# Attention heads on one core: key maxima a tile sooner, the row of -max in tile 6, the merge's last step in two halves

## The chip, the core and the metric

The kernel runs on one core of a Trainium2 chip. The core has five engines with instruction queues of their own: TensorE (PE, matmuls; its weight loads are shown as PEld), VectorE (DVE), ScalarE (ACT), GpSimd (POOL) and SyncE (SP, which here only issues DMAs). The engines run side by side and wait for each other by semaphores; each works through its own queue in order. The metric is the device time of one execution in microseconds (us). Before the change three runs took 3254.74, 3255.23 and 3263.18 us; the median is 3255.23 us.

## The reference, cut to what matters

The program is two whole transformer blocks for 1024 tokens of width 1024: a first block (a recurrent branch and a latent attention branch, then a mixture of experts) and a second (a gated linear recurrence and pooling, then another mixture of experts). The change lies in the attention of the first block. Its core is:

```python
def chunk_causal_attention(q, k, v):
    B, S, H, _ = q.shape                 # S = 1024, H = 16 heads, 96 per head
    scale = QK_HEAD ** -0.5
    outs = []
    for blk in range(S // Q_BLOCK):      # Q_BLOCK = 128
        q0 = blk * Q_BLOCK
        k_end = q0 + Q_BLOCK
        qb = q[:, q0:k_end]
        s = jnp.einsum('bqhd,bkhd->bhqk', qb, k[:, :k_end]).astype(jnp.float32) * scale
        ...                              # mask by chunks of 64
        s = jnp.where(mask, s, -jnp.inf)
        p = jax.nn.softmax(s, axis=-1).astype(v.dtype)
        outs.append(jnp.einsum('bhqk,bkhd->bqhd', p, v[:, :k_end]))
    return jnp.concatenate(outs, axis=1).reshape(B, S, H * V_HEAD)
```

Afterwards the block forms `merged = gates[:, :, 0] * ya + gates[:, :, 1] * yb`, where yb is this attention and ya the recurrent branch, and multiplies it by w_out.

## The kernel before

Everything is float32. A product is made of three matmuls, of operands split into a high and a low part (h and l in the names): high by high, high by low, low by high.

The attention takes the 16 heads one after the other, and each head in 8 key tiles of 128 keys (kt = 0 to 7). Scores are made transposed, with keys in the partitions: `s_mm` (L942) makes for one key tile the scores of all later queries, in pieces of up to 512 columns (tile `st`, three PSUM buffers), and ACT writes their exponential into `raw` (L952; three buffers). `s_split` (L954) makes of raw the high part `ph` (on ACT, for tile 0 on DVE) and on POOL the low part `pl` (L253; from 1024 columns for tile 0 down to 128 for tile 7; three buffers each). Three key tiles later, `av` (L960) multiplies them by the values and adds into two PSUM accumulators of 512 queries (`o`): for each piece it issues value-high by ph, value-low by ph and value-high by pl.

The maxima that the exponential needs are not taken from these scores. While head h is worked on, the next head n = h + 1 is prepared: `t_piece` (L896) transposes its keys and queries in tiles 0 and 1 (tile `tm` in PSUM, three buffers, which is shared by the next two), `m_piece` (L913) makes for a query tile i and 512 keys from a a plain score product (one matmul, L918), and DVE takes its maximum along the keys (L921, and L923 for the diagonal's last 64 keys) into `nm`. `row_piece` (L925) takes the largest of these per query with a minus sign (mz, L927), turns them into a row by eight small matmuls (L931), and ACT (L937) and DVE (L935) copy the row into the queries' tile, as one more contraction row. Then the scores come out with their maximum taken off, and so row_piece stands in front of all scores of head n. `v_piece` (L906) splits the values of head n: DVE the high part (vh, L251), POOL the low part (vl, L253).

The sums of the exponentials come out of the same accumulators. `finish` (L974) copies an accumulator half into y (L985 on DVE for the second half) and sends the row of sums through a small DMA; `rec` (L989) takes the reciprocals and brings them back, over DRAM, spread over 64 partitions, by the DMAs L995 and L998, into the tile `rec`. A pair of heads (2 pr and 2 pr + 1) shares one tile rec of 128 partitions, and the pool has a single buffer of that name: the tile for a new pair is asked for in `rec` of its even head. `merge` (L1000) then works on rec in six parts: parts 0 and 1 multiply by y for either head (POOL, L1006), part 2 takes in one gate (DVE, L1008), part 3 the recurrent branch (DVE, L1010), part 4 writes the high half of the result (ACT, L1013, two instructions), part 5 the low one (DVE, L1016, two instructions) and then starts the loads of the gates for the next pair (`gates`, L1023). When each part comes is in the table MERGE (L832): a first head and a key tile for each part, and then every second head. So part 0 is in tile 6 of odd heads, part 1 in tile 5 of even ones, parts 2 to 5 in tiles 0 to 3 of odd heads from 3 on, for the pair before.

The order is written out by hand. `line` (L1057) yields the units of one step: the pieces of s_mm for (h, kt), then those of av for three tiles earlier; after the last unit come `finish` and `s_split`. (In tile 0 of a head the av of the last head's tile 5 comes first.) `beside` (L1076) gives a list of fillers for that step, in this order: transposes, maxima, the values, the row, rec, the merge. The loop at L1106 to L1129 deals the fillers out evenly among the units:

```python
next(units)
for u in range(nu):
    next(units, None)
    for f, *a in fill[-(-len(fill) * u // nu):-(-len(fill) * (u + 1) // nu)]:
        f(*a)
```

so that how many fillers a step has decides behind which unit each of them comes, and whether it stands before or after the step's s_split.

Of the kernel before, what the change touches and what calls it, by code (L numbers as in the profile page):

```python
# [231 lines left out]
class Body:  # L232
# [601 lines left out]
    def attention(self, rb, rk, ml):  # L834
# [4 lines left out]
        with ExitStack() as cx:  # L839
# [14 lines left out]
            def load(pr):  # L854
                if pr >= 8:
                    return
                if pr not in L:
                    room(pr)
                c, o = pr // 2, pr % 2
                d = L[pr]  # L860
                for w, a in (("k", self.k_d), ("q", self.q_d)):
                    nc.sync.dma_start(d[w][:, :1536].rearrange("p (t c) -> p t c", t=8),
                                      a[c].rearrange("(t p) c -> p t c", p=128)[:, :, o * 192:o * 192 + 192])
                for i, w in enumerate("kq"):
                    nc.sync.dma_start(d[w][:, 1536:].rearrange("p (t c) -> p t c", t=4),
                                      self.v_d[c].rearrange("(t p) c -> p t c", p=128)
                                      [:, i * 4:i * 4 + 4, o * 128:o * 128 + 128])
# [208 lines left out]
            def beside(h, kt):  # L1076

                n = h + 1
                fill = []
                if kt == 0 and h % 2:  # L1080
                    load(h // 2 + 2)
                if n < 16:
                    if kt < 2:
                        fill += [(t_piece, n, "kq"[kt], half) for half in range(2)]
                    fill += [(m_piece, n, i, a) for i, a in
                             {3: [(7, 0), (7, 512), (6, 0)], 4: [(6, 512), (5, 0), (5, 512)],
                              5: [(4, 0), (4, 512), (3, 0)], 6: [(2, 0), (1, 0), (0, 0)]}.get(kt, ())]
                    if kt == 5:
                        fill.append((v_piece, n))
                    if kt == 7:  # L1090
                        fill.append((row_piece, n))
                if kt == 3 and h > 0:
                    fill.append((rec, h - 1))
                for part, (late, at) in enumerate(self.MERGE):
                    if h >= late and (h - late) % 2 == 0 and kt == at:
                        fill.append((merge, (h - late) // 2, part, 0, 2, nc.vector if h == 15 else nc.gpsimd))
                return fill

# [7 lines left out]
            for j in range(16 * 8 + 3):  # L1106
                if j == 13 * 8:
                    wo(0, 3)
                    wo(1, 2)
                if j == 14 * 8 + 6:  # L1110
                    wo(2, 1)
                    wo(3, 0)
                if j == 15 * 8 + 3:
                    rk.close()
                    co = rb.enter_context(tc.tile_pool(reuse_waits="tile", name="co", bufs=1, side="right"))
                    self.cols1 = co.tile([128, 8, 32, 6], BF, name="cols1")
                    wa = rk.enter_context(tc.tile_pool(reuse_waits="tile", name="wa", bufs=1, side="right"))
                if j == 128:
                    last(0)
                units = line(j)  # L1120
                fill = beside(j // 8, j % 8) if j < 128 else []
                if 15 * 8 + 4 <= j < 15 * 8 + 7:
                    fill.append((self.wo_split, wa, *((0, 0), (0, 1), (1, 0))[j - 124]))
                nu = sum(len(chunks(k)) for k in ([j % 8] if j < 128 else []) + ([(j - 3) % 8] if j >= 3 else []))
# [5 lines that stand above are left out]
# [1624 lines left out]
```

## Time and profile before

| | |
|---|---|
| median of three runs | 3255.23 us (3254.74 to 3263.18) |
| the profiled execution | 3259.96 us |
| its span in the profile | 3258.1 us |
| PE busy in the span | 2923.7 us, 90% |
| DVE, ACT, POOL busy | 2002.5, 1395.4, 988.0 us |
| granted TensorE clock, mean | 0.949 of full speed |

The heads of the attention run from about 742 to 1110 us after the start of the span. There each engine's idle time is put down to what ended it, and the time of one head can be read from one group of row matmuls (L931) to the next. PEclk is the share of full clock that TensorE was granted; its two levels are 1.2 and 2.4 GHz, so 0.50 is the lower one. Busy time of an engine that shares a resource with another can be longer than its work.

### The profile page before, as it was taken

The numbers are of one execution on the slowest core, as the hardware profiler recorded it, in microseconds if no ns is written. First come the engines' busy times: TensorE is split into PE (matmuls) and PEld (weight loads), VectorE is DVE, ScalarE is ACT, GpSimd is POOL, SyncE is SP. The second block draws the span as 40 slices with busy tenths as digits, with TensorE's granted clock in tenths as the row PEclk, the third lists the DMA queues.
The fourth block names the chain that finished last, engine by engine and source line by source line (L and its number), as shares of the span: only waits on it lengthen the run. The fifth ranks groups of instructions, "written<-read, shape, count | busy, mean of one in ns | idle before, by whom it ended". The sixth has DMA issues, their size and how long they took to land. (4 is left out here: it accounts for less than half of the span.)

```text
span 3258.1 us, 43717 instructions
## 1 busy us (share of the span) xinstructions
PE 2923.7 (90%) x16309; PEld 2268.3 (70%) x16309; DVE 2002.5 (61%) x3093; ACT 1395.4 (43%) x2096; POOL 988.0 (30%) x678
## 2 busy tenths in 40 slices
PE   5999999998888987899699998857999999999994
PEld 4778778886777885666488878845666666656563
DVE  5554651667877648998645566544655555555456
ACT  3333331545666424776443333332444444444342
POOL 0000000135777414564211132121333333222223
PEclk9999999998999997999899999978999999999997
DMA  3112120353232357999710003337989999999994
GB/s 113 65 56 81 65 88 7 120 163 99 75 88 91 115 204 228 342 349 347 245 52 27 27 17 101 110 128 226 278 278 318 320 322 314 312 310 314 298 287 139
DMA packets 225897, 579.84 MB, mean 178 GB/s; under 512 B 22421, under 2 KB 104005, under 8 KB 225653
## 3 DMA queue, kind: packets, MB, share of 16 engines
q1 hardware_dynamic: 188240, 445.42, 39.0%
q0 software_dynamic: 37008, 131.50, 16.2%
q8 instruction: 131, 2.15, 0.3%
q14 instruction: 86, 0.70, 0.1%
q10 hardware_dynamic: 432, 0.06, 0.0%
HBM read 470.22 MB, written 106.64 MB: 177 GB/s over the span
## 5 line engine op out<-in xcount | busy, mean ns | idle before, releaser
L271 PE MATMUL mm<-uh,wh 128*128 128x512 f32 x640 | 252.7, 395 | 10.8 <-ACT t L505 8.8
L272 PE MATMUL gups<-gl,xh 128*128 128x512 f32 (+1 forms) x608 | 246.9, 406 | 10.4 <-DVE gl L253 10.4
L271 PE MATMUL gups<-gh,xh 128*128 128x512 f32 (+1 forms) x608 | 254.5, 419 | 1.3 <-ACT xh L1594 0.9
L273 PE MATMUL mm<-uh,wl 128*128 128x512 f32 x640 | 251.8, 393 | 0.0
L272 PE MATMUL mm<-ul,wh 128*128 128x512 f32 x640 | 251.6, 393 | 0.0
L273 PE MATMUL gups<-gh,xl 128*128 128x512 f32 (+1 forms) x608 | 246.7, 406 | 0.4 <-DVE xl L1595 0.4
L1696 POOL DMA_INDIRECT acc_d<-y,si x68 | 119.3, 1755 | 408.0 <-DVE y L1693 175.7
L1480 PE MATMUL gups<-raw,x 128*128 128x512 f32 x512 | 226.7, 596 | 0.0
L253 POOL TENSOR_TENSOR pl<-raw,ph 128x1024 fp32r<-128x1024 f32 (+7 forms) x128 | 203.6, 1610 | 71.3 <-ACT ph L247 36.1
L253 DVE TENSOR_TENSOR gl<-raw,gh 128x1024 fp32r<-128x1024 f32 x185 | 217.9, 1219 | 8.0 <-ACT gh L247 7.9
L1627 ACT ACTIVATE th<-gups 128x128 f32<-128x128 f32 (+2 forms) x136 | 49.0, 360 | 349.1 <-PE gups L273 187.2
L247 ACT ACTIVATE gh<-raw 128x1024 fp32r<-128x1024 f32 x188 | 188.5, 1058 | 14.0 <-PE gups L273 12.7
L1584 PEld LDWEIGHTS tp<-ident,xg 128*128 128x128 f32 (+2 forms) x1088 | 112.5, 143 | 97.2 <-issue 36.4
L1691 ACT ACTIVATE y<-yps,wsl 128x512 f32<-128x512 f32 (+1 forms) x100 | 68.8, 688 | 253.1 <-PE yps L273 152.1
L1480 PEld LDWEIGHTS gups<-raw,x 128*128 128x128 f32 x512 | 96.4, 193 | 108.1 <-issue 108.1
L1628 DVE SCALAR_TENSOR_TENSOR hh<-th,gups 128x128 f32<-128x128 f32 (+2 forms) x136 | 52.9, 389 | 186.0 <-ACT th L1627 180.3
L1584 PE MATMUL tp<-ident,xg 128*128 128x128 f32 (+2 forms) x1088 | 128.2, 261 | 42.2 <-DMA xg<-h_d 27.7
L1693 DVE TENSOR_SCALAR y<-yps,wsl 128x512 f32<-128x512 f32 (+1 forms) x95 | 71.1, 748 | 137.5 <-ACT y L1691 137.5
L271 PEld LDWEIGHTS mm<-uh,wh 128*128 128x128 f32 x640 | 121.8, 190 | 38.0 <-ACT t L505 10.6
L272 PEld LDWEIGHTS gups<-gl,xh 128*128 128x128 f32 (+1 forms) x608 | 112.2, 184 | 43.1 <-issue 11.8
L273 PEld LDWEIGHTS mm<-uh,wl 128*128 128x128 f32 x640 | 121.6, 190 | 25.7
L272 PEld LDWEIGHTS mm<-ul,wh 128*128 128x128 f32 x640 | 121.7, 190 | 25.4
(681 smaller groups left out, 8204.3 us busy)
## 6 DMA issues: line engine op xcount, KB each, us to landing
raw<-in_w_down_dram SPq DMA_DIRECT2D x78, 1024.0 KB
raw<-in_w_gate_dram SPq DMA_DIRECT2D x154, 512.0 KB
raw<-in_w_up_dram SPq DMA_DIRECT2D x154, 512.0 KB
w<-in_w_in_dram SPq DMA_DIRECT2D x20, 1024.0 KB
b<-in_w_gate_dram SPq DMA_DIRECT2D x38, 512.0 KB
b<-in_w_up_dram SPq DMA_DIRECT2D x38, 512.0 KB
b<-in_w_down_dram SPq DMA_DIRECT2D x18, 1024.0 KB
w<-in_w_in_dram SPq DMA_DIRECT2D x20, 512.0 KB
```

What stands on the lines that cost most here:

```text
L247: nc.scalar.activation(hi, src, AF.Copy)
L253: e.tensor_tensor(lo, src, hi.bitcast(F32), op=OP.subtract)
L271: nc.tensor.matmul(out, lh, rh, start=start and i == 0, stop=False, **kw)
L272: nc.tensor.matmul(out, lh, rl, start=False, stop=False, **kw)
L273: nc.tensor.matmul(out, ll, rh, start=False, stop=stop and i == n - 1, **kw)
L1480: nc.tensor.matmul(out, x, w, start=start and i == 0, stop=stop and i == len(pairs) - 1, **kw)
L1584: nc.tensor.transpose(ps[:, k // 4, (k % 4) * R:(k % 4) * R + R], xg[:R, k * 128:k * 128 + 128], self.ident[:R, :R])
L1627: nc.scalar.activation(th[:R, :W], ps[:R, 0:W], AF.Tanh, scale=0.5)
L1628: nc.vector.scalar_tensor_tensor(hh[:R, :W], th[:R, :W], 1.0, ps[:R, 0:W], op0=OP.add, op1=OP.mult)
L1691: nc.scalar.activation(y[:R, 0:512], ps[0][:R], AF.Copy, scale=w)
L1693: nc.vector.tensor_scalar(y[:R, 512:1024], ps[1][:R], w, None, op0=OP.mult)
L1696: nc.gpsimd.indirect_dma_start(out=acc_d, out_offset=bass.IndirectOffsetOnAxis(ap=si, axis=0), in_=y[:R], in_offset=None, compute_op=OP.add)
```

## The change

All of it is in `beside`. The maxima of the next head, which stood in tiles 3 to 6 (three a tile), stand in tiles 2 to 5 (two, three, three, four). `row_piece` goes from tile 7 to tile 6, behind a filler that does nothing. `v_piece` goes from tile 5 to tile 7. Part 5 of the merge, in heads below 15, goes from tile 3 to tiles 6 and 7, one half of the queries in each; with its second half go the loads of the next gates. In head 15 nothing of the merge moves.

```diff
                     fill += [(m_piece, n, i, a) for i, a in
-                             {3: [(7, 0), (7, 512), (6, 0)], 4: [(6, 512), (5, 0), (5, 512)],
-                              5: [(4, 0), (4, 512), (3, 0)], 6: [(2, 0), (1, 0), (0, 0)]}.get(kt, ())]
-                    if kt == 5:
+                             {2: [(7, 0), (7, 512)], 3: [(6, 0), (6, 512), (5, 0)], 4: [(5, 512), (4, 0), (4, 512)],
+                              5: [(3, 0), (2, 0), (1, 0), (0, 0)]}.get(kt, ())]
+                    if kt == 6:
+                        fill += [(lambda: None,), (row_piece, n)]
+                    if kt == 7:
                         fill.append((v_piece, n))
-                    if kt == 7:
-                        fill.append((row_piece, n))
                 if kt == 3 and h > 0:
                     fill.append((rec, h - 1))
                 for part, (late, at) in enumerate(self.MERGE):
-                    if h >= late and (h - late) % 2 == 0 and kt == at:
+                    if h < late or (h - late) % 2:
+                        continue
+                    if part == 5 and h < 15:
+                        if kt > 5:
+                            fill.append((merge, (h - late) // 2, part, kt - 6, kt - 5))
+                    elif kt == at:
                         fill.append((merge, (h - late) // 2, part, 0, 2, nc.vector if h == 15 else nc.gpsimd))
```

At three places the order of instructions is shown, each time at the end of head 3, an odd head. First PE, from the last maxima of the next head (L918) to the row matmuls (L931); st are scores, o the accumulators. Before:

```order
L918 MATMUL tm<-kq_4615 128x128
L969 MATMUL o_5580<-ph,vh_4755 128x512
L969 MATMUL o_5580<-ph,vl_4756 128x512
L969 MATMUL o_5580<-pl,vh_4755 128x512
L949 MATMUL st<-kq_4754 128x128
L950 MATMUL st<-kq_4754 128x128
L951 MATMUL st<-kq_4754 128x128
L931 LDWEIGHTS mz
L931 MATMUL tm<-identb,mz 97x128
```

and after:

```order
L918 MATMUL tm<-kq_4615 128x128
L949 MATMUL st<-kq_4754 128x256
L950 MATMUL st<-kq_4754 128x256
L951 MATMUL st<-kq_4754 128x256
L931 LDWEIGHTS mz
L931 MATMUL tm<-identb,mz 97x128
```

Between the last maximum and the row stand now the three score matmuls of tile 6 (256 columns), and no product with the values. In even heads, whose step has one filler less, the three 128-column products with the values of tile 3 stand there too.

Then DVE at the same place: the last maxima, mz, the row's copy, and what follows up to the high part of the next head's tile 0. Before:

```order
L921 TENSOR_REDUCE nm_4609<-tm 128x1
L923 TENSOR_REDUCE nm_4609<-tm 64x1
L927 TENSOR_REDUCE mz<-nm_4609 128x8
L935 CAST kq_4615<-tm 1x512
L260 TENSOR_TENSOR kq_4754<-tm,kq_4754 96x512 x2
L251 CAST ph<-raw 128x1024
```

and after:

```order
L921 TENSOR_REDUCE nm_4609<-tm 128x1
L923 TENSOR_REDUCE nm_4609<-tm 64x1
L927 TENSOR_REDUCE mz<-nm_4609 128x8
L935 CAST kq_4615<-tm 1x512
L1016 SCALAR_TENSOR_TENSOR mgl_4745<-rec,mgh_4744 128x512
L251 CAST vh_4616<-b_4987 128x4x64
L251 CAST vh_4616<-b_4986 128x4x64
L1016 SCALAR_TENSOR_TENSOR mgl_4747<-rec,mgh_4746 128x512
L260 TENSOR_TENSOR kq_4754<-tm,kq_4754 96x512 x2
L251 CAST ph<-raw 128x1024
```

Behind the row's copy stand now the two halves of the last merge step, with the values' high parts between them.

Then POOL from the low part of tile 5 (384 columns) of head 3 to that of the next head's tile 0 (1024); vl is the values' low part, L1006 part 0 of the merge. Before:

```order
L253 TENSOR_TENSOR pl<-raw,ph 128x384
L253 TENSOR_TENSOR vl_4617<-b_4987,vh_4616 128x4x64
L253 TENSOR_TENSOR vl_4617<-b_4986,vh_4616 128x4x64
L253 TENSOR_TENSOR pl<-raw,ph 128x256
L1006 TENSOR_TENSOR rec<-rec,y 64x1024
L253 TENSOR_TENSOR pl<-raw,ph 128x128
L253 TENSOR_TENSOR pl<-raw,ph 128x1024
```

and after:

```order
L253 TENSOR_TENSOR pl<-raw,ph 128x384
L1006 TENSOR_TENSOR rec<-rec,y 64x1024
L253 TENSOR_TENSOR pl<-raw,ph 128x256
L253 TENSOR_TENSOR vl_4617<-b_4987,vh_4616 128x4x64
L253 TENSOR_TENSOR vl_4617<-b_4986,vh_4616 128x4x64
L253 TENSOR_TENSOR pl<-raw,ph 128x128
L253 TENSOR_TENSOR pl<-raw,ph 128x1024
```

L1006, which stood between the pieces of 256 and 128 columns, stands now in front of both, and the values behind the first of them.

## Rows read from the trace of the kernel before

**Rows 1.** The page's first line.

```profile
span 3258.1 us, 43717 instructions
```

**Rows 2.** Per head: us; PE, PEld, DVE, ACT, POOL busy (count); PEclk, DMA, GB/s.

```profile
790.53:809.62 19.09, 17.92 (x108) 15.67 (x108) 13.56 (x31) 13.18 (x25) 13.95 (x10) 1.00 0.07 16
809.62:834.29 24.67, 21.51 (x109) 17.79 (x110) 20.29 (x35) 13.73 (x26) 17.83 (x12) 0.86 0.48 139
834.29:853.34 19.05, 17.88 (x111) 15.63 (x110) 13.63 (x31) 13.61 (x27) 14.85 (x11) 1.00 0.07 16
853.34:877.50 24.16, 20.43 (x109) 16.55 (x109) 20.30 (x35) 14.17 (x27) 17.88 (x13) 0.93 0.47 142
...
1051.51:1070.61 19.10, 17.92 (x108) 15.68 (x109) 13.52 (x31) 13.18 (x25) 14.73 (x11) 1.00 0.08 18
```

**Rows 3.** Waits from 771 to 1071 us: us in all, times, longest.

```profile
PE tm L918 <- DVE nm L923: 16.6, 6, 2.8
...
PE tm L931 <- DVE mz L927: 11.6, 11, 1.9
```

**Rows 4.** The same for SP's queue of DMA issues.

```profile
SPq L998 <- DVE mgl L1016: 16.5, 6, 3.8
```

**Rows 5.** PE's timeline, heads 1 to 3: start us, us, instruction, idle before.

```profile
790.53 0.65 PE L931 MATMUL tm<-identb,mz 128*97 128x128 bf16 x8 [1.94 <-DVE mz L927]
...
809.62 0.65 PE L931 MATMUL tm<-identb,mz 128*97 128x128 bf16 x8 [1.17 <-DVE mz L927]
...
816.01 0.28 PE L969 MATMUL o<-pl,vh 128*128 128x256 f32 x1
...
820.39 0.50 PE L969 MATMUL o<-ph,vh 128*128 128x512 f32 x1 [0.29 <-DVE y L985]
...
827.49 1.10 PE L918 MATMUL tm<-kq 96*128 96x512 f32 x2 [2.77 <-DVE nm L923]
```

**Rows 6.** DVE's timeline from the end of head 2 into head 3.

```profile
807.52 0.49 DVE L921 TENSOR_REDUCE nm<-tm 128x1 f32<-128x320 f32 x1
...
809.38 0.19 DVE L927 TENSOR_REDUCE mz<-nm 128x8 bf16<-128x24 f32 x1
810.31 0.70 DVE L935 CAST kq<-tm 1x512 fp32r<-1x512 f32 x1 [0.74 <-PE tm L931]
...
817.63 2.11 DVE L1010 SCALAR_TENSOR_TENSOR rec<-m,rec 128x1024 f32<-128x1024 f32 x1
...
822.46 4.24 DVE L1016 SCALAR_TENSOR_TENSOR mgl<-rec,mgh 128x512 fp32r<-128x512 f32 x2
...
829.80 0.63 DVE L921 TENSOR_REDUCE nm<-tm 128x1 f32<-128x448 f32 x1
```

**Rows 7.** POOL's timeline where head 2 ends.

```profile
809.82 2.37 POOL L1006 TENSOR_TENSOR rec<-rec,y 64x1024 f32<-64x1024 f32 x1
812.27 1.15 POOL L253 TENSOR_TENSOR pl<-raw,ph 128x256 fp32r<-128x256 f32 x2
815.34 3.31 POOL L253 TENSOR_TENSOR pl<-raw,ph 128x1024 fp32r<-128x1024 f32 x1 [1.92 <-DVE ph L251]
```

**Rows 8.** Line L1016: duration ns min/median/max, first and last start, form.

```profile
L1016 DVE SCALAR_TENSOR_TENSOR mgl<-rec,mgh x16: 692/2108/2331, 822.5 to 1105.7; 128x512 fp32r<-128x512 f32 x16
```

**Rows 9.** One issue of L998, and stretches of 0.5 us after it.

```profile
847.10 0.46 SPq L998 DMA_DIRECT2D rec<-rec_d  x1
...
849.00:849.50 0.50, 0.50 (x5) 0.41 (x4) 0.50 (x2) 0.03 (x1) 0.50 (x1) 1.00 0.59 197
849.50:850.00 0.50, 0.50 (x4) 0.41 (x3) 0.46 (x3) 0.06 (x1) 0.20 (x1) 1.00 0.03 8
```

**Rows 10.** ACT's timeline in tiles 0 and 1 of head 4.

```profile
838.49 1.08 ACT L952 ACTIVATE raw<-st 128x512 f32<-128x512 f32 x2
...
840.65 0.68 ACT L262 ACTIVATE kq<-tm,gk 96x512 fp32r<-96x512 f32 x1
```

**Rows 11.** The stretch behind the 2.77 us.

```profile
827.50:831.00 3.50, 3.50 (x10) 2.74 (x11) 3.25 (x10) 0.28 (x1) 0.32 (x1) 0.50 0.75 249
```

## The prediction

> **What bounds the kernel now.** I took the span first: 3258.1 us, of an execution of 3259.96 us [rows 1]. The sum below is made against that execution; the median of the three runs, 3255.23 us, lies 4.7 us lower, so the change that I find is put on the median at the end. Then I cut the attention at the row matmuls L931, which stand at the end of each head, into one stretch per head [rows 2]: even heads take 19.1 us with PE busy 17.9 of it at the full clock (1.00, the 2.4 GHz level), and the six odd heads from 3 to 13 take 24.2 to 24.7 us at a mean clock of 0.86 or 0.93, three of each. From 809.62 to 1070.61 lie six odd and six even heads, 260.99 us, or 43.5 us for a pair. PE is the bound, and what it waits for is the list of waits [rows 3]: 16.6 us in six waits for DVE's maxima (L923), 11.6 us for the row of maxima (mz, L927). The timeline places them [rows 5, 6]. In each odd head DVE does L1010 and then both halves of the merge's last step (L1016, 4.24 us at one go) in front of the maxima; PE, which has three buffers for them, stands 2.77 us, and the clock then falls to 0.50, the 1.2 GHz level [rows 11]. In each even head PE stands 1.17 us before the row matmuls, since DVE has just begun the last maxima.
>
> **The change part by part.**
>
> *Odd heads.* The last step leaves key tile 3. That takes out the 2.77 us, and with it the slow clock: (1-0.86) x 24.67 = 3.5 us or (1-0.93) x 24.16 = 1.7 us [rows 2], 2.6 us as the mean. What is late next is worked out from DVE's queue. L1010 ends at 819.74 as before (its inputs don't move) [rows 6]. Behind it stand now two maxima more, and PE's fifth maximum product (tile 6, second half) needs the buffer of the first: 819.74 + 0.61 = 820.35. PE would be there at 819.5 (816.01 [rows 5], 0.48 us of that product and the scores behind it, 0.28 us of the wait below, three maximum products of 0.23 us, 2.0 us of scores and values): 0.86 us. The copy L985 comes behind those two maxima, 1.5 us later than before, and PE waits 0.3 us for the accumulator (0.29 before [rows 5]). The first product in tile 2 needs the second half of the queries, which ACT writes last in tile 1 (L262, until 841.33 in head 4 [rows 10]; PE is there 816.49 - 809.62 = 6.9 us after the row matmuls, at 841.1): 0.28 us, in every head. At the end the row matmuls come right behind the scores of tile 6. DVE's chain there is 0.86 us (tile 3's maximum, first row 829.80 and the 64-wide one behind it) and 2.05 us (807.52 to the end of mz at 809.57 [rows 6]), begun 0.8 us into tile 5, so it ends 3.7 us into it; PE gets there after 2.5 us: 1.2 us. An odd head becomes 17.92 + 0.28 + 0.86 + 0.3 + 1.2 = 20.6 us instead of 24.4: **3.8 us gained**.
>
> *Even heads, the row.* There one more product pair (0.3 us) stands in front of the row matmuls, but four maxima instead of three stand in the tile before: 3.7 - 2.8 = 0.95 us instead of 1.17. With the 0.28 us above this is nil. Head 1 waits 1.94 us [rows 5] and head 0 as long; each may gain 0.7 us: 1.4 us. The values' split, now in tile 7, has its first reader in tile 3 of the next head; DVE and POOL do it where POOL idles 1.92 us before its 1024-wide piece [rows 7]: nothing. Nor do the two gate loads cost, which go from tile 3 to tile 7 with the last step: their readers L1008 and L1010 stand a whole head later.
>
> *The new wait.* The tile "rec" has one buffer. In an odd head rec() asks for it in tile 3 for the next pair, so SP's DMA L998 waits until the last reader of the old pair, L1016, is done; the trace shows that wait now, 16.5 us in six times [rows 4], and it is harmless since L1016 follows at once. With the change L1016's second half is in tile 7. So L998 stands in SP's queue from tile 3 to tile 7, behind it only 2 KB pieces and the next gates, not urgent. But POOL's L1006 of the next pair stays in tile 6, reads what L998 brings, and now stands ahead of the 256-wide piece of pl (it stood behind it). Behind L1006 queue that piece, the values, the 128-wide and the 1024-wide piece; PE waits for the first of them in tile 1 of the next head. From the start R of the row matmuls: L935 ends at R + 1.39 (809.62 to 811.01), first half of L1016 0.62, two casts 0.5, second half 0.69: R + 3.2. L998 is issued 0.07 us later. Its data flow until 2.4 to 2.9 us after the issue at 847.10 [rows 9]; I take 2.75: R + 6.05. L1006 2.37, the 256-wide piece 0.73 (812.27 to 813.00, the first of the two [rows 7]), with the hand-overs R + 9.25. PE needs it at R + 7.65: in the trace its product with pl comes 816.01 - 809.62 = 6.39 after R [rows 5], and now 1.26 us of matmuls (two products of tile 3, the scores of tile 7) lie behind R which lay before it. So PE waits 1.6 us. ACT is held too: the raw tile of tile 1 takes the buffer which the 256-wide piece has read, and from there to the end of ACT's last L262 are 2.3 us (839.03 to 841.33 [rows 10]); the first maximum product needs this, at R + 11.65, where PE would be at R + 9.75: 1.9 us more. Less the 0.28 us counted above PE is 1.6 + 1.9 - 0.28 = 3.2 us late. The 1024-wide piece is then ready at R + 13.5 and PE asks for it at R + 15: no third wait. **3.2 us lost** in the next even head, 22.3 instead of 19.1.
>
> Here the length of L1016 decides. It took 2.108 us in the median and 0.692 at the least [rows 8]; POOL works beside it now, and at the change's place it stands still in front of L1006. I take 0.69. The other end is 2 x 1.42 = 2.8 us a pair, 17 us in all. The Trainium skill ("SBUF — State Buffer", section "SBUF: two separate sides") says that a VectorE instruction with two SBUF inputs and a GpSimd one exclude each other for a whole instruction; by it a POOL that waits leaves L1016 alone, and the sum is that with 0.69; without it, with 2.11, it would be 17 us more. The spread of L1016's durations agrees.
>
> *The clock.* The two waits, 1.6 and 1.9 us, have only 0.5 us of matmuls between them. Waits of 1.94 us alone left the clock at full speed [rows 2, 5], those of 2.77 us were followed by half speed each time. Bounds: nothing, and 2.6 us at each of six ends, 15.4 us. The pair of waits is nearer to the 2.77 us row; I take four falls of six, 10.3 us.
>
> *Sum.* 6 x (3.2 - 3.8) = -3.6, heads 0 and 1 -1.4, clock +10.3: about +5.5 us: 3265.5 on the profiled execution, **3261 us** on the median. Nothing else in the program moves; head 15 keeps its merge.
>
> **The rivals.** *Slower: the wait for rec grows heavier.* Place: POOL's L1006 at the end of heads 3 to 13. A gain of 3.8 us stands against 3.2 us and the clock; above 5.7 us a pair the whole is slower by over 0.3%. With the clock falling all six times it is 3.2 + 2.6 = 5.8, +10.6 us, 3266; with L1016 at half-way between its two durations 8 us more, 3274; with both at their ends 3283. For it: one row (2.77) with six falls of six. Against: POOL idles there, and ACT may be free earlier. *Faster: L1006 is covered.* If L1016's second half ends some 3 us earlier against PE, the end of the head costs nothing and the clock stays: 3255 - 6 x 3.8 - 1.4 = 3231, 3241 with half of it. For it: POOL is busy only 14.9 of 19.05 us, 17.8 of 24.67 in an odd head [rows 2]. Against: the path from mz over L998 to the 256-wide piece is 9 us, all in rows, against 7.6 us of matmuls. *The row does not come late any more* (it does what it says): 13 x 0.95 us less, 3249; against it, DVE's 2.9 us of maxima and mz in front. *The clock never falls:* 3250. The Trainium skill ("TensorE: Matmul & The Clock Gate", section "A second HAM failure mode: psum-queue depth-cycling") has a rule that speaks against the change: short idles between groups of matmuls make the clock swing. By it all six ends would fall, the 3266 above. The trace bears it out for 2.77 us and not for the 1.17 us in each even head, at clock 1.00.
>
> **How the numbers follow.** A measurement of this kernel can tell about 0.3%, 9.8 us, from no change. No difference (3261, 3250 and 3249 are all in it): 0.47. Slower, 3266 to 3283: 0.36. Faster, 3231 to 3245: 0.17. The likeliest case alone reaches from 3247 to 3266: -5 us without any fall, +10.6 with all, and 3 us for the landing (0.5 us a pair). The range takes in a part of either rival: at its low end, 3241, half of the 3.2 us and no fall (3261 - 10.3 - 9.6); at its high end, 3281, L1016 at 2.1 us, four falls and a late landing (3261 + 17 + 3).
>
> **What would show it.** Right: PE's wait for L923 of 2.77 us gone and L1016 at 0.69 us; in heads 3 to 13 SP's L998 waits 8 us or more for L1016, POOL L1006 for rec some 5 us, PE for pl about 1.6 us and for ACT's kq (L262) 1.9 us in the next head; odd heads near 20.6 us, even ones from 4 to 14 above 22; mz waits near 1 us. Wrong: no wait of POOL in front of L1006; L1016 still 2.1 us; a clock of 1.00 (or 0.86 everywhere) in the even heads; waits for the row that are gone.

## The result, and the profile after

The changed kernel takes **3286.85 us** (median of 6 runs, 3282.33 to 3295.57); the kernel before took 3257.84 us beside it. The ratio is 1.009, 95% interval 1.0078 to 1.0102: slower by 0.9%, about 29 us, and 6 us beyond the upper end of the predicted range. The profiled run took 3286.02 us, its span 3284.2 us against 3258.1 [rows 1].

Where the time went stands in the heads. The table runs from mz to mz (L927), that is from head to head; columns as in [rows 2].

```profile
809.88:830.34 20.46, 18.41 (x105) 15.22 (x105) 17.67 (x34) 14.36 (x28) 17.83 (x12) 1.00 0.39 104
830.34:856.88 26.54, 22.03 (x111) 18.65 (x111) 14.92 (x33) 13.16 (x25) 14.06 (x12) 0.87 0.18 61
...
924.17:951.30 27.13, 22.97 (x111) 19.32 (x111) 14.92 (x33) 13.15 (x25) 14.07 (x12) 0.81 0.17 58
951.30:971.77 20.47, 18.41 (x105) 15.23 (x105) 17.67 (x33) 14.37 (x28) 17.83 (x12) 1.00 0.38 104
```

Odd heads (first and last row), which took 24.2 to 24.7 us [rows 2], take 20.5. Even heads, which took 19.1, take 26.5 and 27.1 here and 26.3 to 27.5 in all six, at a clock of 0.87 or 0.81 instead of 1.00. To split this into waiting and slower work, the same table was summed over the six heads of a kind, in each kernel: first the six even heads from 4 to 14, then the six odd ones from 3 to 13. First the kernel after:

```profile
sum 161.96, PE 136.18 PEld 114.76 DVE 89.45 ACT 78.93 POOL 84.75; mean PE 22.70 PEld 19.13 DVE 14.91 ACT 13.16 POOL 14.12
...
sum 122.81, PE 110.47 PEld 91.24 DVE 106.01 ACT 86.12 POOL 107.02; mean PE 18.41 PEld 15.21 DVE 17.67 ACT 14.35 POOL 17.84
```

And the kernel before:

```profile
sum 114.83, PE 108.55 PEld 94.89 DVE 81.39 ACT 81.39 POOL 87.89; mean PE 18.09 PEld 15.82 DVE 13.56 ACT 13.57 POOL 14.65
...
sum 146.15, PE 124.70 PEld 102.38 DVE 121.79 ACT 82.71 POOL 108.19; mean PE 20.78 PEld 17.06 DVE 20.30 ACT 13.79 POOL 18.03
```

The stretch is "sum", PE's work is "PE", the difference is PE's idle time. Odd heads: 146.15 to 122.81, -23.3 us. Even heads: idle from 6.3 (114.83 - 108.55) to 25.8 us (161.96 - 136.18), +19.5; and PE's work from 108.6 to 136.2 us, +27.6. Not all of the last is the clock. With the row in its new place an even head holds 111 matmuls from mz to mz and an odd one 105, where each held some 108. A kernel with the same order on PE, whose clock stays at 1.00 (rec freed early, below), gives the six even heads at full clock:

```profile
sum 117.37, PE 112.48 PEld 96.70 DVE 99.60 ACT 78.96 POOL 88.35; mean PE 18.75 PEld 16.12 DVE 16.60 ACT 13.16 POOL 14.73
```

So 3.9 of the 27.6 us (112.48 - 108.55) are there without any fall of the clock, and 23.7 (136.18 - 112.48) are the clock. Odd and even heads together: +23.8. The rest of the 26.1 us lies outside these heads: -1.4 in heads 0 to 2, +1.9 ahead of the first row, where nothing was changed, +1.8 behind the last.

The waits of PE in heads 3 to 14, after (us in all, times, longest):

```profile
PE o L969 <- POOL pl L253: 13.1, 6, 2.4
PE tm L931 <- DVE mz L927: 9.1, 12, 1.3
PE tm L918 <- ACT kq L262: 8.5, 6, 1.4
...
PE tm L918 <- DVE nm L923: 2.4, 6, 0.4
```

The wait for the maxima, 16.6 us in six times [rows 3], is down to 2.4. In its place stand two new ones, six times each: for POOL's pl and for ACT's kq. Their chain at the end of head 3, engine by engine. DVE (start, duration):

```profile
832.00 0.69 DVE L1016 SCALAR_TENSOR_TENSOR mgl<-rec,mgh 128x512 fp32r<-128x512 f32 x1
...
833.01 0.68 DVE L1016 SCALAR_TENSOR_TENSOR mgl<-rec,mgh 128x512 fp32r<-128x512 f32 x1
```

SP, which had stood at this DMA since tile 3 (39.4 us in six times, at most 6.8, instead of the 16.5 of [rows 4]), and POOL:

```profile
833.73 0.46 SPq L998 DMA_DIRECT2D rec<-rec_d  x1
```

```profile
829.43 0.99 POOL L253 TENSOR_TENSOR pl<-raw,ph 128x384 fp32r<-128x384 f32 x1 [0.84 <-PE st L951]
837.83 2.34 POOL L1006 TENSOR_TENSOR rec<-rec,y 64x1024 f32<-64x1024 f32 x1 [7.42 <-PE st L951]
840.14 0.71 POOL L253 TENSOR_TENSOR pl<-raw,ph 128x256 fp32r<-128x256 f32 x1
```

ACT, whose raw tile takes the buffer that this piece of pl has read:

```profile
840.89 0.49 ACT L952 ACTIVATE raw<-st 128x384 f32<-128x384 f32 x1 [4.09 <-POOL pl L253]
...
842.32 0.69 ACT L262 ACTIVATE kq<-tm,gk 96x512 fp32r<-96x512 f32 x1
```

PE:

```profile
840.91 0.39 PE L969 MATMUL o<-pl,vh 128*128 128x256 f32 x1 [2.41 <-POOL pl L253]
...
843.06 0.80 PE L918 MATMUL tm<-kq 96*128 96x512 f32 x1 [1.41 <-ACT kq L262]
```

POOL stands 7.42 us in front of L1006 (the row puts this down to PE, whose st was long there; L1006 began 4.1 us after L998's issue). L1016 is down from 2.1 us [rows 8] to 0.69. PE gets its pl at 840.91, works 0.7 us, and stops again for kq. The clock falls at about that time. Such stretches of half clock, measured to 0.1 us, in head 4 and in head 8, after:

```profile
842.80:849.70 6.90, 6.64 (x19) 5.60 (x20) 4.40 (x8) 3.63 (x7) 6.00 (x3) 0.51 0.02 4
935.00:945.20 10.20, 8.79 (x26) 7.11 (x25) 5.94 (x11) 5.11 (x10) 7.29 (x6) 0.50 0.00 0
```

And in heads 3 and 5, before:

```profile
827.00:833.80 6.80, 6.31 (x21) 5.39 (x22) 5.60 (x18) 1.51 (x3) 3.19 (x4) 0.50 0.55 193
871.40:874.80 3.40, 3.40 (x11) 2.58 (x11) 3.16 (x10) 0.37 (x1) 0.14 (x1) 0.50 0.77 270
```

After the change the stretch lasts 6.9 us in heads 4 and 6 and 10.2 in heads 8 to 14. What the clock takes is half of PE's work in it, since in the longer ones PE also stands idle: 2 x 3.3 + 4 x 4.4 = 24 us, the 23.7 above.

The fall does not stand at the same place each time. The clock just ahead of PE's second wait in head 8, that wait, and the clock right behind the same wait in head 6:

```profile
935.02:935.14 0.12, 0.12 (x2) 0.00 (x0) 0.00 (x0) 0.12 (x1) 0.12 (x2) 0.50 0.00 0
```

```profile
936.55 0.80 PE L918 MATMUL tm<-kq 96*128 96x512 f32 x1 [1.41 <-ACT kq L262]
```

```profile
889.82:890.64 0.82, 0.82 (x4) 0.70 (x5) 0.82 (x2) 0.82 (x2) 0.82 (x1) 1.00 0.00 0
```

In heads 8 to 14 the clock falls within 0.15 us of the start of the wait for kq, so nearly all of this wait comes after the fall and can't have brought it on. In head 4 it falls 0.2 us before this wait ends, and in head 6 0.8 us behind it.

### The profile page after: what moved, and what is told of

It is laid out like the page before. It is cut to its first block, busy times and chain, and to the rows that moved or that the text cites. A ratio compares the mean times of both kernels' runs of the same rounds, so it can differ in the third digit from the quotient of the medians.

```text
span 3284.2 us, 43712 instructions
## 1 busy us (share of the span) xinstructions
PE 2936.2 (89%) x16309; PEld 2277.2 (69%) x16309; DVE 1994.5 (61%) x3093; ACT 1394.5 (42%) x2096; POOL 982.4 (30%) x678
## 5 line engine op out<-in xcount | busy, mean ns | idle before, releaser
L253 DVE TENSOR_TENSOR gl<-raw,gh 128x1024 fp32r<-128x1024 f32 x185 | 217.8, 1218 | 8.5 <-ACT gh L247 8.4
L253 POOL TENSOR_TENSOR pl<-raw,ph 128x1024 fp32r<-128x1024 f32 (+7 forms) x128 | 195.5, 1539 | 67.5 <-ACT ph L247 44.8
```

Of the source, the lines that this page charges most:

```text
L253: e.tensor_tensor(lo, src, hi.bitcast(F32), op=OP.subtract)
```

## The experiments

The ratios are to the kernel before, run beside each. "Theory" is the chain just shown: L1016 in tile 7, L998, L1006, pl, PE and ACT, then the clock.

**One part alone: the merge's last step.** The kernel before, with only this part of the change:

```diff
-                    if h >= late and (h - late) % 2 == 0 and kt == at:
+                    if h < late or (h - late) % 2:
+                        continue
+                    if part == 5 and h < 15:
+                        if kt > 5:
+                            fill.append((merge, (h - late) // 2, part, kt - 6, kt - 5))
+                    elif kt == at:
```

> The kernel before with only the merge's last step moved (halves in tiles 6 and 7); maxima, row and values as before. Theory (the wait for rec): L998 waits until tile 7, POOL for rec some 7 us, even heads 26 to 27 us at 0.81 to 0.87; odd heads 20.5 to 21.5 us since L1016 no longer stands in tile 3, the halves now among the last maxima and the row: 3283 to 3292 us. Rival (the loss comes from the earlier maxima or the row's move): even heads 19.1 us and odd heads below 21.5: 3240 us.

Measured: 3279.32 us, ratio 1.0066 (1.0047 to 1.0085). Heads 3, 4 and 8:

```profile
811.17:832.61 21.44, 18.45 (x108) 15.51 (x108) 17.78 (x34) 14.15 (x27) 17.28 (x12) 0.99 0.37 99
832.61:858.30 25.69, 22.49 (x108) 19.35 (x108) 14.31 (x34) 13.16 (x25) 15.02 (x11) 0.81 0.18 63
...
926.99:950.51 23.52, 20.31 (x108) 17.13 (x108) 15.83 (x34) 13.06 (x25) 15.02 (x11) 0.93 0.20 68
```

This part by itself brings most of the gain of the odd heads (21.4 us) and makes the even ones long, so the earlier maxima and the row's move are not needed for a loss. The time is 4 us below the expected range, and the even heads are 23.5 to 26.4 us, some below the expected 26. But it is not the same loss. PE's waits from 811 to 1090 us, and a stretch at the start of head 4:

```profile
PE tm L931 <- DVE mz L927: 23.9, 13, 2.6
PE o L969 <- POOL pl L253: 9.9, 6, 2.6
```

```profile
832.30:835.60 3.30, 2.75 (x13) 2.46 (x14) 1.89 (x4) 0.90 (x2) 0.00 (x0) 0.50 0.00 0
```

The row is still in tile 7 here, and L1016's first half stands in front of mz: PE waits 2.6 us for the row at the end of every odd head, and at the end of five of the six the clock falls, for 3.4 us (6.8 at the start of head 12). There is no wait for kq. About the end of the wait for pl it falls in heads 4 and 6, for 6.8 us, and in head 14 for 10.2. So only a part of this loss is the chain above.

**The other parts alone.** The changed kernel, with that step back in tile 3:

```diff
-                    if part == 5 and h < 15:
-                        if kt > 5:
-                            fill.append((merge, (h - late) // 2, part, kt - 6, kt - 5))
-                    elif kt == at:
+                    if kt == at:
```

> The changed kernel with the merge's last step back in tile 3 in one piece; maxima, row and values stay where the change put them. Theory (the wait for rec): no wait of POOL for rec, even heads 19.1 to 19.3 us at clock 1.00; but L1016 takes 2.1 us a half again beside POOL and stands among the maxima, so that a wait of PE for them of 1.5 to 2.8 us comes back in odd heads with a fall of the clock, 23 to 24.4 us: 3250 to 3257 us, as before the change. Rival (the earlier maxima bring the odd head's gain by themselves): odd heads 20.5 us, 3240 us. Rival (density): even heads keep a low clock, 3267 us or more.

Measured: 3253.08 us, ratio 0.9986 (0.9972 to 0.9999). Heads 3, 4 and 9:

```profile
808.24:830.58 22.34, 20.02 (x108) 16.81 (x108) 18.95 (x36) 14.46 (x28) 18.00 (x12) 0.92 0.50 153
830.58:849.81 19.23, 18.42 (x108) 15.79 (x108) 13.76 (x31) 13.01 (x25) 14.66 (x12) 1.00 0.05 16
...
932.81:955.31 22.50, 18.91 (x108) 15.59 (x108) 20.17 (x35) 14.45 (x28) 18.57 (x12) 1.00 0.50 134
```

No loss in even heads, and a smaller gain in odd ones. Two points were missed. L1016's second half takes 0.69 us in heads 3 to 7, where POOL has hardly begun or stands still, and 2.07 us in heads 9 to 13, where POOL's L253 runs beside all of it; 2.1 us were expected everywhere. Both halves in heads 3 and 9:

```profile
823.71 1.24 DVE L1016 SCALAR_TENSOR_TENSOR mgl<-rec,mgh 128x512 fp32r<-128x512 f32 x2
...
948.29 2.63 DVE L1016 SCALAR_TENSOR_TENSOR mgl<-rec,mgh 128x512 fp32r<-128x512 f32 x2
```

And the odd heads are 22.3 to 22.5 us, not 23 or more. PE's waits there are 1.3 us at the longest, not 1.5 to 2.8; behind such a wait the clock fell for 3.4 us in heads 3, 5 and 7 and not in heads 9, 11 and 13.

**PE kept busy through the two waits.** Matmuls by a zero matrix that add nothing to the accumulator; POOL, ACT and SP wait as before.

```diff
+            def busy(h, n):
+                for _ in range(n):
+                    nc.tensor.matmul(O[h][1], zero, V[h % 2]["h"][:, 0:4], start=False, stop=False, skip_group_check=True)
 ...
+                        if i == 2 and kt == 6 and h in range(3, 15, 2):
+                            busy(h, 10)
 ...
+                if (i, a) == (7, 0) and h in range(5, 16, 2):
+                    busy(h - 2, 6)
```

> The changed kernel with matmuls of zeros (10 of 512 columns in front of the product with pl that waits in tile 1, 6 in front of the maximum product that waits in tile 2 of even heads) which add nothing to the output accumulator; all waits of POOL, ACT and SP stay. Theory (the waits cost 3.3 us and the clock, falling behind them, 4.6 us): PE is busy through both waits, the clock stays 1.00, even heads 22.4 to 22.7 us, 3287 - 27 = 3260 us. Rival (density or another cause of the fall): the clock is 0.81 to 0.87 in even heads all the same, 3285 to 3290 us.

Measured: 3260.75 us, ratio 1.0011 (1.0000 to 1.0023), 26 us less than the changed kernel. Head 4, and PE's work in it (L900 are the zeros; the lines behind them have moved, L969 is L981 and L918 is L928):

```profile
826.72:849.95 23.23, 22.51 (x127) 18.92 (x127) 14.65 (x34) 13.07 (x25) 14.20 (x12) 1.00 0.21 69
```

```profile
834.73 2.50 PE L900 MATMUL o<-vh,zero 128*128 128x512 f32 x10
837.07 0.31 PE L981 MATMUL o<-pl,vh 128*128 128x256 f32 x1
...
837.58 1.55 PE L900 MATMUL o<-vh,zero 128*128 128x512 f32 x6
839.14 0.50 PE L928 MATMUL tm<-kq 96*128 96x512 f32 x1
```

The useful matmuls come as late as before, to within 0.3 us, the clock stays at 1.00 in all six even heads, and the clock's term is gone: six times 23.2 to 23.5 us instead of 26.3 to 27.5. That is 22 us; the rest lies in the main ahead of head 3, where the two kernels differ by a tile of zeros alone, so the expected 3260 us was met in part by luck. The fall follows from PE's standing still, not from the denser odd heads or the work around it.

**Only the second wait filled.**

```diff
-                            busy(h, 10)
+                            busy(h, 0)
```

> The changed kernel with the 6 matmuls of zeros only in front of the maximum product in tile 2 (1.4 us filled), none in front of the product with pl. The wait for pl of 2.0 to 2.4 us stands alone. Theory (the two waits together bring the clock down): the clock stays 1.00 in even heads from 4 to 14, 23.2 us each, 3260 us. Rival (the first wait is enough): the clock falls in all six, for a shorter or equal stretch, 25 to 27 us each, 3272 to 3287 us.

Measured: 3272.66 us (one run). Heads 4 and 10, and one stretch of half clock in head 10:

```profile
828.97:852.12 23.15, 20.43 (x117) 17.18 (x117) 14.63 (x33) 13.04 (x25) 14.36 (x12) 1.00 0.21 69
...
960.60:985.03 24.43, 21.69 (x117) 18.50 (x117) 14.74 (x33) 13.04 (x25) 14.16 (x12) 0.93 0.20 66
```

```profile
971.10:974.50 3.40, 3.40 (x11) 2.82 (x11) 1.49 (x2) 2.94 (x6) 3.40 (x4) 0.50 0.00 0
```

In the heads this lies between the two expectations; the time, of a single run, can't decide, since of its 12 us above the kernel with both waits filled only 2.7 lie in heads 3 to 14. With the wait for pl alone (12.9 us in six times; 13.1 in the changed kernel) the clock stays in four heads and falls in heads 10 and 14, for 3.4 us each. So behind both waits, 0.7 us of work apart, the clock fell six times for 6.9 or 10.2 us, and behind the first alone twice for 3.4. How the second wait does this is not shown: in heads 8 to 14 of the changed kernel the clock had fallen by about its start, and a kernel with only the first wait filled was not run.

**rec freed early.** Step 3 of the merge writes into g1, whose values step 2 has used up, and steps 4 and 5 read it there; rec is free from tile 1 on. (A second buffer for rec does not fit: the pool would need 60.1 KB a partition, 57.3 are left.)

```diff
-                r = d["r"]
+                r = d["g1" if part > 3 else "r"]
 ...
-                    nc.vector.scalar_tensor_tensor(r[:, sl], d["m0"][:, sl], 0.5,
+                    nc.vector.scalar_tensor_tensor(d["g1"][:, sl], d["m0"][:, sl], 0.5,
```

> The changed kernel, but the merge's step 3 writes its sum into the tile g1 (whose values step 2 has used up) and steps 4 and 5 read it there; the tile rec is free from tile 1 of the odd head on, as many instructions of the same sizes as before. Theory (the wait for rec): SP's L998 does not wait for L1016, POOL's L1006 starts at once, PE's waits for pl (2.0 to 2.4 us) and kq (1.4 us) go and with them the fall of the clock; odd heads 20.5 us, even heads 19.2: 3287 - 6 x 7.8 = 3240 us. Rival (order on POOL): L1006 of 2.3 us ahead of the 256-wide piece makes PE wait about 1 us all the same, even heads 20.2 us: 3246 us. Rival (the clock falls for some other reason): even heads 23.7 us, 3267 us.

Measured: 3242.59 us, ratio 0.9942 (0.9922 to 0.9961). Heads 3 and 4, then POOL at the end of head 3:

```profile
809.34:829.79 20.45, 18.41 (x105) 15.20 (x105) 17.67 (x33) 14.35 (x28) 17.82 (x12) 1.00 0.42 117
829.79:849.36 19.57, 18.75 (x111) 16.11 (x111) 16.45 (x34) 13.17 (x25) 14.73 (x12) 1.00 0.21 69
```

```profile
830.08 2.38 POOL L1006 TENSOR_TENSOR rec<-rec,y 64x1024 f32<-64x1024 f32 x1 [0.21 <-DVE mz L927]
832.42 0.74 POOL L253 TENSOR_TENSOR pl<-raw,ph 128x256 fp32r<-128x256 f32 x1
```

The theory's number, within 3 us. L1006 starts at once, both new waits of PE are gone, the clock is 1.00, and the gain in the odd heads stays whole. Even heads are 19.6 us against 19.2 forecast, but L1006 ahead of the 256-wide piece is no wait of PE in this trace.

**L1006 out of the way instead.** POOL's L1006 in tile 2 of the next even head; L998 waits as in the changed kernel.

```diff
-    MERGE = (1, 6), (2, 5), (3, 0), (3, 1), (3, 2), (3, 3)
+    MERGE = (2, 2), (2, 5), (3, 0), (3, 1), (3, 2), (3, 3)
```

> The changed kernel with the merge's step 0 (POOL's L1006 of the even head's half) in tile 2 of the next even head instead of tile 6 of the odd one; rec still has one buffer, so SP's L998 still waits for L1016 until tile 7. Theory (what costs is POOL standing in front of L1006 with pl behind it): nobody waits for rec any more, even heads 19.2 to 19.5 us at clock 1.00, odd ones 20.0 to 20.5: 3238 to 3243 us. Rival (SP's queue, held by L998 until tile 7, delays the 2 KB pieces or the gates): waits elsewhere, 3250 us or more. Rival (L1006 in tile 2 delays pl there by its 2.3 us): even heads 21 us, 3251 us.

This table leaves the step out for the last pair, which has no next even head. The merge's values are then other ones, and behind the heads the program does other work (44159 instructions in all instead of 43712, 3645.51 us, ratio 1.1185), presumably since the tokens are routed otherwise. Only heads 3 to 14 can be read. Heads 3 and 4:

```profile
807.76:828.22 20.46, 18.70 (x108) 15.55 (x108) 17.68 (x34) 14.34 (x28) 17.83 (x12) 1.00 0.38 104
828.22:847.44 19.22, 18.42 (x108) 15.80 (x108) 15.58 (x33) 13.00 (x25) 14.73 (x12) 1.00 0.25 84
```

No wait of PE for pl or kq, clock 1.00.

**And the row one unit later.** Three kernels with a second free unit ahead of the row: with rec freed early, with L1006 moved (the last pair's kept in tile 6), with both.

```diff
-                        fill += [(lambda: None,), (row_piece, n)]
+                        fill += [(lambda: None,), (lambda: None,), (row_piece, n)]
 ...
+                    if part == 0 and h < 15:
+                        late, at = 2, 2
```

> As the kernel whose step 3 writes into g1, and with two free units instead of one ahead of the row, so that the row comes after the second unit of tile 6 in odd heads and after the third in even ones. Theory: PE's wait for mz (1.2 us in even heads, 0.3 us in odd ones) goes down to near nothing: about 6 x 1.5 us less than the kernel with g1 alone, 3231 us. Rival: the row's copies end later by one unit (1 us), and the first scores of the next head wait for them instead: no difference, 3240 us. Rival: the moved fillers push L1016's first half and L1006 by a unit, so that L1006 delays the 256-wide piece: 3245 us.

> The changed kernel with POOL's L1006 for pairs 0 to 6 in tile 2 of the next even head (the last pair's stays in tile 6 of head 15) and two free units ahead of the row; rec keeps its one buffer and SP's L998 its wait for L1016 until tile 7. Theory (only POOL standing in front of L1006 costs, not SP's wait): even heads 19.2 us, odd ones 20.1, no wait of POOL for rec: 3232 to 3237 us, level with the kernel that writes step 3 into g1 and has the later row. Rival (SP's blocked queue shows up elsewhere): 3245 us or more.

> The kernel whose step 3 writes into g1, with two free units ahead of the row and L1006 for pairs 0 to 6 in tile 2 of the next even head. Theory: L998's wait is gone and POOL does not wait, so there is nothing left to gain over either alone: 3232 to 3237 us. Rival (L1006 at the end of the odd head still held pl, as even heads of 19.6 us against 19.2 suggest): 2 us less than either.

Measured, in this order: 3235.77 us, ratio 0.9920 (0.9903 to 0.9937); 3236.55 us, 0.9914 (0.9893 to 0.9935); 3236.16 us, 0.9912 (0.9891 to 0.9934). Heads 3 and 4 of the second, and its queue of SP:

```profile
806.85:826.99 20.14, 18.50 (x108) 15.29 (x107) 17.55 (x33) 14.39 (x28) 17.82 (x12) 1.00 0.40 106
826.99:846.18 19.19, 18.43 (x109) 15.97 (x110) 15.68 (x33) 13.01 (x25) 14.75 (x12) 1.00 0.24 84
```

```profile
SPq L998 <- DVE mgl L1016: 47.4, 7, 7.9
```

All three beat both kernels, and between them there is no difference. In the second SP still stands 47.4 us in seven times at L998, and nobody pays for it: what cost was POOL in front of L1006 with pl behind it, not the DMA queue. The row's later place is worth little: the medians with rec freed early are 7 us apart (3242.59 and 3235.77; 9 were expected), but the intervals of the ratios overlap, and in the traces heads 3 to 14 are 2.9 us shorter.

## Why the prediction was wrong

- **The odd head's gain: right, in part by luck.** 3.8 us were forecast, 22.8 over six; the rows show 23.3. L1016 at 0.69 us, the 2.77 us wait gone: as written. But of the 2.6 us of waits in the forecast's 20.6 the trace shows 1.8 (0.6 for the maxima, 1.2 for the row; none for kq or L985), and PE's work is 18.4 us, not 17.9; the two errors cancel. L1016 takes 0.69 us where POOL stands still, and in the kernel whose last step went back to tile 3 it takes 0.69 us where POOL has hardly begun and 2.07 beside its L253. The Trainium skill ("SBUF — State Buffer", section "SBUF: two separate sides") says that a VectorE instruction with two SBUF inputs and a GpSimd one that reads SBUF exclude each other for a whole instruction; these lengths agree with it.
- **The new wait: right in its place and its chain, nearly in size.** Its pieces were off in both directions. L1016's second half ended 3.1 us after the row's matmuls began (3.2 forecast), but L1006 began 4.1 us after L998's issue, not 2.75: the end of the traffic [rows 9] is not yet the start of the reader (the trace after has L998's data landed 3.3 to 4.0 us behind the issue). So PE waited 2.0 to 2.4 us for pl instead of 1.6. For kq it waited 1.4 instead of 1.9. Together that is 3.6 us against 3.5. But without the clock's part an even head became some 4 us longer (23.2 to 23.5 us with the waits filled), not 3.2: it also waits 0.4 us for the last maxima and holds 0.65 us more of PE's work, against 0.9 us less at the row.
- **The clock: the step that failed.** "I take four falls of six, 10.3 us": there were six, and they cost some 24 us (23.7 by PE's work, 22 by the kernel with the waits filled). Two falls more at 2.6 us are 5 us of the difference; the other 8 are the price of one, 4.0 us instead of 2.6. These 13 us are most of what lies between the +5.5 us of the sum (its terms give +5.3) and the +26.1 of the trace; 4 more lie in the even heads at full clock and 4 outside heads 3 to 14. 2.6 us a fall was the mean of what single waits leave in the kernel before, 3.4 and 6.8 us of half clock, 1.7 and 3.4 us lost. Here the stretch lasts 6.9 or 10.2 us, 3.3 or 4.4 us lost. The prediction weighed the pair between a wait of 1.94 us alone and one of 2.77, as if the price of a fall were one figure and only its frequency open; its own upper end had no room for a longer stretch. The length of the longest wait does not order the falls either: with the last step back in tile 3 the clock fell three times of six behind 1.3 us. That the clock's term hangs on the waits is shown with the waits filled; that filling the second is not enough, with one of them filled. Why the stretches are longer than before the change stays open.
- **The rivals.** "Slower: the wait for rec grows heavier" is what happened, with six falls; a pair then lost 3.9 us at full clock and 4.0 us by the clock against a gain of 3.9. Its ways to 3283 (a slower L1016) had no part. The Trainium skill ("TensorE: Matmul & The Clock Gate", section "A second HAM failure mode: psum-queue depth-cycling") says of another kernel that short idles of PE between groups of matmuls make the clock swing; how long a fall lasts that section does not say. The six falls agree with it; falls in two and in three heads of six, in the kernels with the second wait filled and with the last step back, show that not each such wait is followed by one.
- **The small terms: nearly right.** Heads 0 to 2 gave 1.4 us. The row still comes late, 1.2 us at the end of odd heads, as forecast, and 0.3 at the end of even ones instead of 0.95.

## What to carry to other kernels

When the last reader of a one-buffer tile is moved later, look up which instruction asks for the tile next and what queues behind the instruction that reads its new contents; here two lines, which let a used-up tile take the sum, turned a loss of 0.9% into a gain of 0.6%. Price a wait of PE with the clock behind it: in this kernel two waits close together cost as much in clock as in waiting (4.0 and 3.6 us a head). And when a fall of the clock has been seen at two lengths, its price is a range, not a mean, and may lie above both.

## What the runs showed of the hardware

The half-clock stretch differed in length behind like waits: 6.9 us in heads 4 and 6 and 10.2 us in heads 8 to 14, behind a wait for pl of 2.0 to 2.4 us and one of 1.4 us for kq in each. In heads 8 to 14 the wait for kq lies in the stretch, in heads 4 and 6 it lies ahead of nearly all of it; but a stretch of 10.2 us also followed a wait for pl of 2.6 us without one for kq (head 14 of the kernel with the last step alone). What decides between the lengths was not found. Nor did the longest wait decide whether the clock falls: behind 2.77 us it fell six times of six, behind 2.0 to 2.4 us alone twice of six, behind 1.3 us three times of six, and behind 1.94 us at the ends of heads 0 and 1 before the change [rows 5] not at all. PE was at work in most of such a stretch (8.79 of 10.20 us in head 8), so its return to full clock did not follow at once from being busy. From the issue of L998 to the start of the POOL instruction that waited for its data 4.1 us passed, though the traffic belonging to a like DMA had ended some 2.4 to 2.9 us behind its issue [rows 9]; the landing of L998's data is 3.3 to 4.0 us behind it in the trace after.
